# The first half of SwiGLU_1 in a staircase of four column groups, with the first two conditioning columns summed by TensorE

## The chip, the cores and the metric

The kernel runs on one core of one Trainium2 chip. The metric is device time in microseconds (us), the median of several runs; the time before is 1943.49 us (three runs, 1943.44 to 1944.72). The engines that matter are TensorE (PE, with its weight loads PEld), VectorE (DVE), ScalarE (ACT) and SyncE (SP), whose queue issues all DMA transfers. Each engine takes its instructions strictly in the order in which they stand in its queue. A scheduler fixes that order when the kernel is built; it is free to place instructions that do not depend on each other otherwise than the code writes them.

## The reference

One decoder layer on 256 tokens of width 2048 in float32. Only its first step is touched:

```python
mod = silu(c) @ ada_w + ada_b                  # 9 x 2048 numbers: shift, scale, gate of three stages
h = rmsnorm(x) * norm_g * (1 + sc1) + sh1      # 256 x 2048
x = x + 0.5 * gt1 * ((silu(h @ wg) * (h @ wu)) @ wd)   # wg, wu: 2048 x 5632, wd: 5632 x 2048
```

A mixer (two groups of heads), a second SwiGLU and a final norm follow.

## The kernel before, in words

Features lie on the 128 partitions: h is 16 tiles of 128 features x 256 tokens, numbered k = 0 to 15. Each of the two weight matrices wg and wu is cut into tiles of 128x128, k by f (f = 0 to 43 is a column of 128 hidden features). To keep float32 accuracy with the faster rounded type, each weight tile is split into a rounded part `whi` and a remainder `wlo`, and each h tile into a part HI and a part LO, so a weight tile costs three matmuls of 128x256: hi times HI (L567), hi times LO (L568), lo times HI (L569).

Weights arrive in blocks of eight tiles (512 KB, `Stream.block`, L112 to 124): SP issues the DMA into `wraw` (five buffers in this stage), ACT rounds it into `whi` (L123, four buffers), DVE subtracts to make `wlo` (L135, four buffers). A buffer of `whi` or `wlo` is free again when PE has read its last tile. The order in which `next` is called for tiles (L126) is the order of the blocks; the host packs them so.

The conditioning columns come the same way: a column is 128 output features of `mod`, 1 MB of `ada_w`; DVE multiplies it with silu(c) and sums it (L260, one custom instruction). Tile k of h needs two columns, scale and shift of its 128 features; then DVE multiplies x by the gain and the norm's row (`ht`, L368), ACT adds the shift and rounds (L375; L370 and L371 for odd k), and DVE makes the LO part (L376, L372). `RATE` says how many columns are loaded per block; `ada_need` forces a column that the code is about to use.

SwiGLU_1's gate and up products are made in two halves; the first half, 28 columns f, is `gate_up_first`. It makes them before all of h exists. A PSUM bank (of eight) holds g and u of one f. `CHUNKS` cuts the 16 tiles k into 0-1, 2-7 and 8-15; in each chunk a first group of eight f is worked k by k (`LEAD` says for how many k), then f by f, then the other f singly. When an f's chunk is finished its bank is emptied at once (`evacuate`): after the first chunk ACT copies it to an accumulator (L580), after the second DVE adds it (L582), after the third DVE adds gate and up to it for the activation (L585).

Before the first product stands a head, in which everything of the start is made: PE does ten warm-up matmuls on zeros, spreads c over the partitions by four one-row matmuls (`pcs`, L658), transposes x (`px`, L679), and turns the norm's reciprocal into a row (`nrow`, L709); ACT squares x (`junk`, L673), makes silu(c) (`cs`, L662) and copies PSUM to x (L681); DVE computes the reciprocal root and sums the first two columns, each in two halves (L694).

## Time and profile before

| what | value |
|---|---|
| median of three runs | 1943.49 us |
| profiled execution | 1943.79 us, its span 1941.9 us |
| PE busy | 1903.0 us, 98% of the span |
| DVE busy | 1554.0 us, 80% |
| ACT busy | 1041.2 us, 54% |
| first product of SwiGLU_1 (first L567) | starts at 22.52 us |
| last product of its first half (last L569) | starts at 336.8 us |
| DMA, mean over the span | 268 GB/s |

Busy time is the union of an engine's instructions; PE at 98% leaves little idle time, and nearly all of what the change can touch lies in the first 340 us. The time outside the span (1.9 us) is launch and end.

### The profile page before, as it was taken

Reading aid. Unit: us, or ns where it says so; the run is one execution under the profiler, and the core shown is the slowest. Engines: PE = TensorE matmul, PEld = TensorE weight load, DVE = VectorE, ACT = ScalarE, POOL = GpSimd, SP = SyncE. Lnnn points to the kernel's source line nnn. Section 1 sums busy time; section 2 is a strip of 40 time slices with the busy share of each in tenths; the row PEclk is TensorE's granted clock in tenths of the full one; section 3 lists DMA queues with packets and bytes.
Section 4 is the critical chain, followed back from the end, with each engine's and each line's share of the span. In section 5 each row is a group of like instructions: output and inputs, shape, how many; then the busy total and the mean of one; then the engine's idle time right before and its main releaser. Section 6 shows DMA issues by size and latency. Waiting matters only on the chain. (4 is left out here: it accounts for less than half of the span.)

```text
span 1941.9 us, 33701 instructions
## 1 busy us (share of the span) xinstructions
PE 1903.0 (98%) x13087; PEld 1777.2 (92%) x13087; DVE 1554.0 (80%) x2415; ACT 1041.2 (54%) x1647; POOL 56.8 (3%) x55
## 2 busy tenths in 40 slices
PE   8999999999999999999999999999999999999998
PEld 6999999998999988889989998999999999999997
DVE  6999978989989997779987989976777665666654
ACT  6544555433455446858657655665554445555553
POOL 0000000000000030000000001100000000000011
PEclk8999999999999999999999999999999999999999
DMA  9989867999999975586667568667767665565663
GB/s 371 359 308 358 305 224 258 400 369 376 356 358 339 361 302 212 212 314 220 214 242 257 201 218 303 208 258 252 245 253 257 244 225 200 201 200 202 202 200 120
DMA packets 129490, 519.58 MB, mean 268 GB/s; under 512 B 18217, under 2 KB 21545, under 8 KB 111153
## 3 DMA queue, kind: packets, MB, share of 16 engines
q1 hardware_dynamic: 129330, 517.42, 72.9%
q8 instruction: 103, 1.69, 0.3%
q14 instruction: 57, 0.47, 0.1%
HBM read 512.89 MB, written 4.47 MB: 266 GB/s over the span
## 5 line engine op out<-in xcount | busy, mean ns | idle before, releaser
L135 DVE TENSOR_TENSOR wlo<-wraw,whi 128x1024 fp32r<-128x1024 f32 x674 | 822.3, 1226 | 268.3 <-ACT whi L123 267.3
L123 ACT CAST whi<-wraw 128x1024 fp32r<-128x1024 f32 x674 | 700.6, 1047 | 515.1 <-PE pd L485 166.5
L485 PE MATMUL pd<-hid,whi 128*128 128x512 f32 x1408 | 461.8, 382 | 0.0
L486 PE MATMUL pd<-hid,wlo 128*128 128x256 f32 x1408 | 384.6, 273 | 2.6 <-DVE wlo L135 2.6
L260 DVE CUSTOM_DVE_ANT_0 adat<-adat,cs,colt 128x2048 f32<-128x2048 f32 x140 | 329.2, 2351 | 6.5 <-DMA adat<-in_ada_dram 6.5
L481 PE MATMUL pg<-hs,whi 128*128 128x512 f32 x912 | 302.2, 382 | 0.5 <-DVE shc L432 0.5
L481 PE MATMUL pu<-hs,whi 128*128 128x512 f32 x912 | 302.2, 382 | 0.0
L485 PEld LDWEIGHTS pd<-hid,whi 128*128 128x128 f32 x1408 | 266.0, 189 | 36.9
L486 PEld LDWEIGHTS pd<-hid,wlo 128*128 128x128 f32 x1408 | 270.3, 192 | 5.4 <-DVE wlo L135 5.3
L567 PE MATMUL pgu<-hs,whi 128*128 128x256 f32 x896 | 245.8, 277 | 5.9 <-ACT hs L371 5.9
L482 PE MATMUL pu<-hs,wlo 128*128 128x256 f32 x912 | 249.2, 273 | 0.0
L482 PE MATMUL pg<-hs,wlo 128*128 128x256 f32 x912 | 248.9, 273 | 0.0
L569 PE MATMUL pgu<-hs,wlo 128*128 128x256 f32 x896 | 245.1, 278 | 2.4 <-DVE wlo L135 2.4
L568 PE MATMUL pgu<-hs,whi 128*128 128x256 f32 x896 | 246.5, 277 | 0.0
L481 PEld LDWEIGHTS pg<-hs,whi 128*128 128x128 f32 x912 | 172.4, 189 | 24.8 <-ACT shc L431 0.7
L481 PEld LDWEIGHTS pu<-hs,whi 128*128 128x128 f32 x912 | 172.4, 189 | 23.6
L769 PE MATMUL pp<-hs,whi 128*128 128x256 f32 x656 | 188.9, 289 | 1.6 <-ACT hs L375 1.6
L770 PE MATMUL pp<-hs,whi 128*128 128x256 f32 x656 | 182.9, 279 | 0.0
L771 PE MATMUL pp<-hs,wlo 128*128 128x256 f32 x656 | 182.7, 278 | 0.0
L567 PEld LDWEIGHTS pgu<-hs,whi 128*128 128x128 f32 x896 | 172.9, 194 | 6.7 <-ACT hs L371 6.3
L482 PEld LDWEIGHTS pu<-hs,wlo 128*128 128x128 f32 x912 | 175.0, 192 | 1.0 <-DVE wlo L135 0.9
L482 PEld LDWEIGHTS pg<-hs,wlo 128*128 128x128 f32 x912 | 175.1, 192 | 0.4
(337 smaller groups left out, 2593.8 us busy)
## 6 DMA issues: line engine op xcount, KB each, us to landing
wraw<-in_w_dram SPq DMA_DIRECT2D x674, 512.0 KB, 4.4
adat<-in_ada_dram SPq DMA_DIRECT2D x140, 1024.0 KB, 7.2
xr<-in_xr_dram SPq DMA_DIRECT2D x4, 512.0 KB, 5.3
adaf<-in_ada_dram SPq DMA_DIRECT2D x4, 512.0 KB, 8.5
adaf<-in_ada_dram SPq DMA_DIRECT2D x2, 1024.0 KB, 12.3
xd<-x SPq DMA_DIRECT2D x4, 512.0 KB, 7.0
rw<-rowd SPq DMA_DIRECT2D x16, 128.0 KB, 4.3
x<-xd SPq DMA_DIRECT2D x4, 512.0 KB, 5.8
```

Source lines behind the costliest of these rows:

```text
L123: self.cast = self.nc.scalar.copy(self.h, r).ins
L135: lo_ = nc.vector.tensor_tensor(self.l, r, self.h.bitcast(F32), ALU.subtract)
L260: V.tensor_tensor_reduce(t, t, cs, 1.0, L("adab", q, 1), ALU.mult, ALU.add, mod[:, q : q + 1])
L481: PE.matmul(ps, wt[0], both, start=(k == 0), stop=False)
L482: PE.matmul(ps[:, T:], wt[1], part(k, HI), start=False, stop=(k == KD - 1))
L485: PE.matmul(ps, wt[0], act.rearrange("p q (a b) -> p q b a", a=2), start=first, stop=False)
L486: PE.matmul(ps[:, :T], wt[1], woven(act[:, 0]), start=False, stop=last)
L567: PE.matmul(o, wh, part(k, HI), start=first and s == 0, stop=False, skip_group_check=skip)
L568: PE.matmul(o, wh, part(k, LO), start=False, stop=False, skip_group_check=skip)
L569: PE.matmul(o, wl, part(k, HI), start=False, stop=last, skip_group_check=skip)
L769: PE.matmul(pp[i][:, :T], wh, hh, start=(k == 0), stop=False)
L770: PE.matmul(pp[i][:, :T], wh, hl, start=False, stop=False)
```

## The change

It has five parts.

1. `CHUNKS` and `LEAD` give way to `PIECES`, thirteen rows (group, first k, k up to which the group is worked k by k, end k) over groups of 8, 8, 8 and 4 columns f. The number of blocks is the same (112); the first blocks use k = 0 alone for two groups, the third group brings in k = 1, the fourth k = 2, and so on. There are 13 pieces where group and chunk gave 12; 28 banks are copied by ACT as before, 32 are added in the middle by DVE where there were 28.
2. A bank is no longer emptied when its piece is finished, but when the next piece asks for it (`owed`), except in pieces that end f by f.
3. Head: the first two columns (`first_col`) are summed by TensorE, sixteen 128x1 float32 matmuls each, with silu(c) as a column `csk` that sixteen one-row 128x1 matmuls `pct` prepare. The second half of `cs` is made after the first rounded weights; block 0 is rounded and subtracted in two halves; two and two warm-up matmuls stand where seven stood.
4. A later column is summed by DVE one block after the block with which it was loaded (`W.late`, `lag`), and `RATE` is 0.5 columns per block up to block 12 and then 0.45 up to block 68, where it was 0.5 up to 24, 0.34 up to 56 and 0.45 up to 68.
5. The rows of `ada_w` for the first two columns are packed so that TensorE can take them as stationary operand.

```diff
-CHUNKS = (0, 2, 8, 16)
-LEAD = (2, 5, 5)
+PIECES = (
+    (0, 0, 1, 1), (1, 0, 1, 1), (2, 0, 2, 2), (3, 0, 3, 3), (0, 1, 4, 4), (1, 1, 6, 6), (3, 3, 7, 7),
+    (2, 2, 11, 11), (3, 7, 12, 12), (0, 4, 11, 16), (1, 6, 6, 16), (2, 11, 11, 16), (3, 12, 12, 16),
+)
-RATE = ((0, 0.5), (24, 0.34), (56, 0.45), (68, 0.06), (112, 0.5), (168, 0.38), (264, 0.0), (284, 0.26), (404, 0.0), (424, 0.125))
+RATE = ((0, 0.5), (12, 0.45), (68, 0.06), (112, 0.5), (168, 0.38), (264, 0.0), (284, 0.26), (404, 0.0), (424, 0.125))
-N_WARM = (10, 7)
+N_WARM = (10, 2, 2)
...
-        self.cast = self.nc.scalar.copy(self.h, r).ins
+        with nullcontext() if b != 1 else self.tc.issue_after(self.lead):
+            one, *more = self.pieces(b)
+            h = self.h
+            self.cast = self.nc.scalar.copy(h[:, one], r[:, one]).ins
+            self.rest += [lambda q=q: self.nc.scalar.copy(h[:, q], r[:, q]).ins for q in more]
...
             with self.tc.issue_after(lo_.ins):
-                self.settle(b - BEHIND)
+                self.settle(b - self.lag)
...
-        for ci, (k0, k1) in enumerate(chunks):
...
+        for g, k0, ks, k1 in PIECES:
+            grp = fs[8 * g : 8 * g + 8]
+            pb = {}
+
+            def both(f, k):
+                ada_need(0, k)
+                if f not in pb:
+                    if len(owed) == 8:
+                        owed.pop(0)()
+                    pb[f] = bank()
+                for s in range(2):
+                    three(pb[f], f, s, k, k0, k1)
+
+            for k in range(k0, ks):
+                for f in grp:
+                    both(f, k)
+            for f in grp:
+                for k in range(max(k0, ks), k1):
+                    both(f, k)
+                owed.append(lambda f=f, ps=pb[f], k0=k0, k1=k1: evacuate(ps, f, k0, k1))
+                while ks < k1 and len(owed) > 1:
+                    owed.pop(0)()
+        while owed:
+            owed.pop(0)()
...
+    spread(0, psb)
+    spread(1, psb)
+    pct = psf("pct")
+    for k in range(KD):
+        PE.matmul(pct[:, k : k + 1], crow[:, k * P : (k + 1) * P], one[:1, :1], start=True, stop=True)
...
-    for kind, i in (("x", 0), ("x", 1), ("c", 0), ("c", 1), ("x", 2), ("x", 3), ("c", 2), ("c", 3)):
+    for kind, i in (("x", 0), ("x", 1), ("c", 0), ("c", 1), ("k", 0), ("x", 2), ("x", 3)):
...
+            elif kind == "k":
+                hold = A.activation(csk, pct[:, :KD], AF.Silu).ins
...
+        for k in range(KD):
+            PE.matmul(pcol[:, i : i + 1], first_ada[i][:, k * P : (k + 1) * P], csk[:, k : k + 1], start=(k == 0),
+                      stop=(k == KD - 1), skip_group_check=True)
+        return V.tensor_tensor(mod[:, q : q + 1], pcol[:, i : i + 1], L("adab", q, 1), ALU.add)
```

How the order moves on three engines follows. The first place is PE's queue in the head, between the ten warm-up matmuls and the first product. Before:

```order
L658 MATMUL pcs<-crow,one 128x512 x4
L679 MATMUL px<-colt,xr 128x128 x24
L709 MATMUL nrow<-colt,frb 128x128 x2
L679 MATMUL px<-colt,xr 128x128 x8
L201 LDWEIGHTS zw
L201 MATMUL zp<-zw 128x512
```

Now (`pct` is c as a column, `pcol` the sum of a conditioning column, `adaf_118` the first of the two; after these rows come one more warm-up matmul, the sixteen `pcol` matmuls of the second column `adaf_119`, two warm-up matmuls and the first product):

```order
L685 MATMUL pct<-one,crow 128x1 x16
L709 MATMUL px<-colt,xr 128x128 x12
L720 MATMUL pcol<-csk,adaf_118 128x1 x3
L709 MATMUL px<-colt,xr 128x128 x8
L720 MATMUL pcol<-csk,adaf_118 128x1 x5
L709 MATMUL px<-colt,xr 128x128 x5
L720 MATMUL pcol<-csk,adaf_118 128x1 x8
L736 MATMUL nrow<-colt,frb 128x128 x2
L709 MATMUL px<-colt,xr 128x128 x7
L679 MATMUL pcs<-crow,one 128x512 x2
L213 LDWEIGHTS zw
```

Forty-eight float32 matmuls of one column moved onto PE ahead of the first product, and two of the four `pcs` moved behind the norm's row.

The second place is ACT's queue from the first rounded h tile on (`whi` is a rounded weight block, `acc` the copy that empties a bank, `hs` the rounding of an h tile). Before:

```order
L375 ACTIVATE hs<-ht,mod 128x2x128
L123 CAST whi<-wraw 128x1024 x3
L370 ACTIVATE ht<-ht,mod 128x256
L371 CAST hs<-ht 128x2x128
L580 COPY acc<-pgu 128x512
L123 CAST whi<-wraw 128x1024
L580 COPY acc<-pgu 128x512 x3
L123 CAST whi<-wraw 128x1024
L580 COPY acc<-pgu 128x512 x5
L123 CAST whi<-wraw 128x1024
```

Now:

```order
L132 CAST whi<-wraw 128x512
L389 ACTIVATE hs<-ht,mod 128x2x128
L133 CAST whi<-wraw 128x512
L690 ACTIVATE cs<-pcs 128x512 x2
L132 CAST whi<-wraw 128x1024 x5
L598 COPY acc<-pgu 128x512 x4
L389 ACTIVATE hs<-ht,mod 128x2x128
L598 COPY acc<-pgu 128x512 x6
L132 CAST whi<-wraw 128x1024
L598 COPY acc<-pgu 128x512 x4
```

The rounding of h tile 1 moved from ahead of all bank copies to between the fourth and the fifth, and the first copy stands behind the rounding of block 5.

The third place is DVE's queue where a group of eight banks is emptied by additions for the first time. Before (the eight additions stand between the remainders of blocks 25 and 26; a pair of L260 rows is one column):

```order
L135 TENSOR_TENSOR wlo<-wraw,whi 128x1024
L372 TENSOR_TENSOR hs<-ht,hs 128x2x128
L135 TENSOR_TENSOR wlo<-wraw,whi 128x1024
L582 TENSOR_TENSOR acc<-pgu,acc 128x512 x8
L135 TENSOR_TENSOR wlo<-wraw,whi 128x1024
L260 ISA adat,mod<-adat,cs,colt 128x2048
```

Now (`wlo_928`, `wlo_963` and `wlo_994` are the remainders of blocks 18, 19 and 20; `pgu_679`, `694`, `701`, `708`, `715` are banks of f = 0 to 4):

```order
L146 TENSOR_TENSOR wlo_928<-wraw_924,whi_926 128x1024
L382 SCALAR_TENSOR_TENSOR ht_892<-x_85,g1_890,nrow_236 128x256
L600 TENSOR_TENSOR acc_363<-pgu_679,acc_363 128x512
L600 TENSOR_TENSOR acc_2634<-pgu_694,acc_2634 128x512
L395 SCALAR_TENSOR_TENSOR hs_127<-ht_892,mod_126,hs_127 128x2x128
L146 TENSOR_TENSOR wlo_963<-wraw_959,whi_961 128x1024
L272 ISA adat_930,mod_126<-adat_930,cs_86,colt_87 128x2048
L272 ISA mod_126 128x1
L146 TENSOR_TENSOR wlo_994<-wraw_990,whi_992 128x1024
L600 TENSOR_TENSOR acc_2636<-pgu_701,acc_2636 128x512
L600 TENSOR_TENSOR acc_2638<-pgu_708,acc_2638 128x512
L600 TENSOR_TENSOR acc_2640<-pgu_715,acc_2640 128x512
```

The additions are now split up: after two of them stand an h tile, two remainders and a column, then five more. On PE the products of the next piece that need the banks still to be emptied are placed behind those of block 19 for f = 8 and 9.

More of the change, by code (lines that the diff above doesn't have):

```diff
@@ L101, in __init__, with settle @@
         self.first = []
-        self.late, self.owing = False, []
-    def settle(self, upto=N_TILES):
+        self.lead, self.rest = None, []
+        self.late, self.owing, self.lag, self.pin = False, [], 1, None
+    def settle(self, upto):
         while self.owing and self.owing[0][0] <= upto:
-            self.owing.pop(0)[1]()
+            self.owing.pop(0)[2]()
     def behind(self, later=True):
@@ L272, in ada_need @@
             ada_col()
-        W.settle()
+        with nullcontext() if W.pin is None else tc.issue_after(W.pin):
+            while W.owing and W.owing[0][1] <= ada_seq.index((m, j)):
+                W.owing.pop(0)[2]()
     W.side = ada_col
@@ L374, in modulate_one @@
             with tc.issue_after(W.cast) if W.first else nullcontext():
-                A.activation(hh, tt, AF.Identity, bias=sh)
+                i = A.activation(hh, tt, AF.Identity, bias=sh).ins
+            if W.first:
+                for later in W.rest:
+                    with tc.issue_after(i):
+                        i = later()
+                W.lead = i
             return V.scalar_tensor_tensor(hl, tt, sh, hh.bitcast(F32), ALU.add, ALU.subtract)
@@ L557, in gate_up_first @@
         W.hold, W.held = None, [ada_done[0, 0]().ins]
-        groups = [fs[i : i + 8] for i in range(0, len(fs), 8)]
-        chunks = list(zip(CHUNKS[:-1], CHUNKS[1:]))
+        W.late = True
         acc, hids = {}, []
@@ L651, in ffn, with spread @@
             W.more = None
-    pcs = []
-    for q in range(4):
-        pcs.append(psn(q + 1, "pcs"))
+    pcs = {}
+    def spread(q, bank):
+        pcs[q] = bank("pcs")
         PE.matmul(pcs[q], one[:1], crow[:, q * 512 : (q + 1) * 512], start=True, stop=True)
+    spread(0, psb)
[3 more added lines that the diff above has]
+        PE.matmul(pct[:, k : k + 1], crow[:, k * P : (k + 1) * P], one[:1, :1], start=True, stop=True)
+    csk = ep.tile([P, KD], F32, name="csk")
     def cond(q):
@@ L711, in layer_kernel @@
     hold = A.copy(first_row, pr[:, :T]).ins
-    for i in range(4, KD // 2):
+    for i in (6, 7):
         features(i)
+    spread(2, pss)
+    spread(3, pss)
     with tc.issue_after(nr.ins):
         warm_up(N_WARM[1])
-    W.first.append(W.block(0))
-    first_col(0, 1)
-    first_col(1, 0)
-    first_col(1, 1)
+    first_col(1)
+    warm_up(N_WARM[2])
+    with tc.issue_after(hold):
+        W.first.append(W.block(0))
+    W.rest += [lambda q=q: cond(q) for q in (2, 3)]
     ada_st["i"] = 2
@@ L1244, in step @@
                     rowf[h + 1] = row_of(h + 1, 0, "f")
-        W.late = True
+        W.lag = 2
         first = project([("gt", 0)] + [("qkv", NH + h) for h in range(3)])
```

70 lines of the change are left out of this document (23 added, 47 removed).

## The prediction

> **What bounds the kernel now.** I read the page's first part, then stretches of the span, then what PE waits for, then the head in order of time.
>
> ```profile
> span 1941.9 us, 33701 instructions
> PE 1903.0 (98%) x13087; PEld 1777.2 (92%) x13087; DVE 1554.0 (80%) x2415; ACT 1041.2 (54%) x1647; POOL 56.8 (3%) x55
> ```
>
> PE bounds the span, so only its idle time and its slow stretches can be won or lost. The next view gives the busy time of each engine in some stretches; the last three columns are the granted clock, the share of the DMA engines and GB/s.
>
> ```profile
> 6.07:9.49 3.42, 3.42 (x9) 1.19 (x8) 0.00 (x0) 3.21 (x8) 0.00 (x0) 1.00 1.03 391
> 9.49:12.90 3.41, 3.41 (x17) 3.41 (x17) 1.53 (x4) 2.94 (x8) 0.00 (x0) 0.50 1.03 376
> 12.90:16.31 3.41, 1.06 (x10) 0.81 (x8) 3.31 (x12) 1.28 (x3) 0.00 (x0) 1.00 1.01 412
> 16.31:19.73 3.42, 2.56 (x12) 2.56 (x13) 2.62 (x9) 1.31 (x4) 0.00 (x0) 0.50 1.03 431
> 19.73:23.14 3.41, 3.41 (x11) 1.60 (x10) 1.00 (x2) 3.31 (x6) 0.00 (x0) 0.50 1.01 422
> 29.97:33.38 3.41, 1.28 (x9) 1.11 (x10) 3.41 (x5) 0.94 (x2) 0.00 (x0) 1.00 0.99 413
> 33.38:36.79 3.41, 3.41 (x19) 3.41 (x18) 3.19 (x5) 2.61 (x4) 0.00 (x0) 0.50 1.04 435
> 150.00:200.00 50.00, 50.00 (x450) 50.00 (x450) 49.07 (x58) 21.97 (x25) 0.00 (x0) 1.00 0.94 354
> ```
>
> In the last row 450 matmuls take 50 us: 0.111 us each, 2.67 us for a block (24). There DVE is busy 49 of 50 us, so it is a close second. The clock moves in steps of 3.41 us: after a stretch with little PE work (1.28 us) the next runs at half.
>
> ```profile
> L567 PE MATMUL pgu<-hs,whi x896: 275/275/765, 22.5 to 336.5; 128*128 128x256 f32 x180
> L569 PE MATMUL pgu<-hs,wlo x896: 274/275/423, 24.6 to 336.8; 128*128 128x256 f32 x180
> ```
>
> Three lines of 896 make 2688 matmuls, at 0.111 us 298.7 us; they take 336.8 + 0.3 - 22.5 = 314.6. **The first half loses 15.9 us, and its first product starts at 22.5 us.** These two numbers are what the change can alter. What PE waits for in the first 330 us, besides clock:
>
> ```profile
> PE pgu L567 <- ACT hs L371: 5.9, 2, 3.6
> PE pgu L569 <- DVE wlo L135: 2.4, 4, 1.5
> ```
>
> That is two h tiles that came late (3.6 and 2.3, with half clock behind them) and remainders `wlo` that came late.
>
> **The head: start of the first product.** From the order of time:
>
> ```profile
> 5.61 3.91 PE L658 MATMUL pcs<-crow,one 1*128 1x512 f32 x8
> 9.45 4.51 PE L679 MATMUL px<-colt,xr 128*128 128x128 f32 x24
> 18.18 1.92 PE L679 MATMUL px<-colt,xr 128*128 128x128 f32 x8
> 741.30 0.51 PE L323 MATMUL nsum<-colt,sqacc 128*128 128x2 f32 x4
> 10.12 1.06 ACT L673 ACTIVATE junk<-xr 128x1024 bf16<-128x1024 f32 x1 [0.47 <-DMA xr<-in_xr_dram]
> 11.08 0.18 ACT L673 ACTIVATION_READ_ACCUMULATOR junk<-xr 128x1 f32 x1
> 11.17 1.07 ACT L662 ACTIVATE cs<-pcs 128x512 f32<-128x512 f32 x2
> 12.13 2.05 ACT L681 COPY x<-px 128x512 f32<-128x512 f32 x4
> 18.42 0.37 ACT L711 COPY nrow<-nrow 128x256 f32<-128x256 f32 x1 [4.25 <-PE nrow L709]
> 11.83 1.28 DVE L694 CUSTOM_DVE_ANT_0 adaf<-adaf,cs,colt 128x1024 f32<-128x1024 f32 x1
> 16.63 0.16 DVE L292 SCALAR_TENSOR_TENSOR rsy_n<-rsa_n,rsy_n 128x2 f32<-128x2 f32 x1
> 16.82 0.48 DVE L708 TENSOR_SCALAR frb<-one,rsy_n 128x128 f32<-128x128 f32 x2
> 21.55 0.56 ACT L375 ACTIVATE hs<-ht,mod 128x256 fp32r<-128x256 f32 x1
> 22.52 1.10 PE L567 MATMUL pgu<-hs,whi 128*128 128x256 f32 x4
> ```
>
> A float32 matmul that is no transpose shows as two records (four `pcs` are eight). The four nsum records end 0.51 us after the first starts, of which one record's 0.25 is drain: about 0.11 us apart, though each has only two columns. A 128x1 matmul is then 2 x 0.11 = 0.22 us at full clock, and 0.43 at half (transposes go from 0.11 to 0.21: eight in 1.92 at half, with the last one's drain). That row is the nearest there is for `pct` and `pcol`.
>
> The Trainium skill, page "TensorE: Matmul & The Clock Gate", section "Back-to-back issue gap", gives a floor of about 25 ns between matmuls of at most 64 columns; the nsum row, four times that, decides here, as each record there brings its own weight load. By the page's floor a column would be 0.8 us in place of 3.6, and the sum would be that of rival (d), 1944.0.
>
> PE's queue, step by step: two `pcs` (four records of 0.43) end at 7.6. `pct`, 32 records, takes 3.6 us at full clock; but the row 6.07:9.49 shows that one-row matmuls that keep PE busy for 3.42 us leave the next stretch at half, so from 9.49 the other 16 take 3.4: end 12.8. Behind it stands ACT: silu of `csk`, which before did not exist, and behind that the last two squares (the last began at 10.12 before), which now end at 15.8 (from 13.4, 1.06 and most of a read each). The x copies at 0.51 follow and free banks from 16.3 on. PE meanwhile: 12 transposes to 15.4, three `pcol` to 16.6. From here the clock matters. At full: eight transposes as the copies free banks, 17.4; five `pcol` 18.5; five transposes 19.05; eight `pcol` 20.85; `nrow` 21.3 (DVE's eleven small operations of 0.19 from 15.9 on and the 0.48 behind them end at 18.5, hidden); seven transposes 22.1; two `pcs` 23.8; two warm-ups 24.25; sixteen `pcol` 27.8; then PE's drain and DVE's addition of the bias 0.45, and ACT's rounding 0.56: **first product at 28.8, 6.3 us later than before**. The same with full clock throughout (9.49 too) gives 27.0; with half clock from 16.6 on, 39.3 (8 and 5 and 7 transposes 4.3, 13 `pcol` 5.5, `nrow` 0.85, `pcs` 3.4, warm-ups 0.85, `pcol` 6.8, end 1.0). I take 28.8: a `pcol` loads weights in all 128 rows, where a `pcs` has one. Both ends stay for the range. The four half sums of 1.28 that DVE loses, 5.1 us, stood on this path too, between its small operations; that gain is in the times above, and PE's new work outweighs it.
>
> The Trainium skill, same page, section "Part 1: The HAM clock gate", says that the clock follows how busy PE has been; by it 27.0 would hold, 1.8 us less. The row 6.07:9.49 (all busy, half clock next) speaks against it.
>
> **After the start.** Durations, copies and additions of a bank first:
>
> ```profile
> L580 ACT COPY acc<-pgu x28: 568/587/619, 33.4 to 66.9; 128x512 f32<-128x512 f32 x28
> L582 DVE TENSOR_TENSOR acc<-pgu,acc x28: 682/688/697, 99.1 to 187.7; 128x512 f32<-128x512 f32 x28
> L123 ACT CAST whi<-wraw x674: 1027/1047/1093, 20.1 to 1919.0; 128x1024 fp32r<-128x1024 f32 x169
> 22.54 2.36 DVE L135 TENSOR_TENSOR wlo<-wraw,whi 128x1024 fp32r<-128x1024 f32 x2
> 24.81 2.35 DVE L260 CUSTOM_DVE_ANT_0 adaf<-adaf,cs,colt 128x2048 f32<-128x2048 f32 x1
> 30.57 0.48 DVE L368 SCALAR_TENSOR_TENSOR ht<-x,g,nrow 128x256 f32<-128x256 f32 x1
> 30.96 1.22 DVE L135 TENSOR_TENSOR wlo<-wraw,whi 128x1024 fp32r<-128x1024 f32 x1
> ```
>
> From start to start on DVE a remainder is 1.14 (two in 24.81 - 22.54), a column 2.27 (its next stands at 27.08), `ht` 0.39. Times now count from the first product.
>
> Blocks 0 and 1: the rounding of block 1 stands behind the second half of block 0 and two `cs` (0.53 + 1.06 + 1.05 = 2.65), its remainder is ready at 3.9; PE ends at 6.1 instead of 5.3: 0.8.
>
> Block 2 needs the bank of f = 0. Its copy stands on ACT behind the rounding of block 5, whose buffer PE frees only when it ends block 1: 0.1 + 1.05 + 0.59 + 0.1 = 1.9 of idle PE.
>
> Block 3 needs the fifth copy, behind the rounding of h tile 1. That needs `ht`, and DVE has ahead of it, from 2.65 on, five remainders 5.7, two columns 4.55, gain and `ht` 0.5: 13.4; rounding to 14.1, copy to 14.7. PE is through block 2 at 10.55: 4.1. Then ACT, with 16 copies (9.4) and the roundings of blocks 6 and 7 among them, is late twice more, 0.5 and 0.7.
>
> Block 17, where eight banks are to be added. Until then PE is not held up (h tiles 2 and 3 are ready 4 and 6 us early). Let PE end block 16 at 0. DVE's queue there: remainder 18, `ht`, two additions, an h tile, remainder 19, a column, remainder 20, addition 3: 8.6 us. Remainder 18 could begin at -4.2 (its buffers come free at -5.3), but a column keeps DVE until -3.1; so addition 3 ends at 5.5, at best 4.4. PE has f = 8 and 9 of blocks 17 and 19 to do, 2.7: idle 2.8 (1.7 at best). The eighth addition stands behind another remainder and column: 0.5 more. Likewise at block 27 (second addition behind a remainder, a column, a remainder: 5.2 after the first, PE has 1.3 of work and DVE 2.0 of lead) 1.9; at block 31 (addition 4 behind four remainders and a column) 2.3; at block 54, 1.9. Together 3.3 + 1.9 + 2.3 + 1.9 = 9.4. The bounds of this term: 0 if DVE leads by its four `wlo` buffers everywhere, 15 if each place costs what 17 does with its clock.
>
> Half clock: the gap of 4.1 is longer than the 2.1 us of idleness in 29.97:33.38, so one stretch of half clock, 1.7. The switch to the next product at 336 shows 1.1 of the 15.9 and stays.
>
> Sum after the start: 0.8 + 1.9 + 4.1 + 1.2 + 9.4 + 1.7 + 1.1 = 20.2 where there were 15.9: **4.3 lost**.
>
> Edits with one answer: `RATE` and the one-block lag move the same 30 columns on DVE; four more additions are 2.8 us of DVE, in the places above; on SP the column of h tile 1 stands two weight blocks later, hidden by the later start (the queue runs at a full DMA share from 6 us on). After the first half the order differs only locally; the largest wait for a remainder there is small, so I count 0, within 1 either way.
>
> ```profile
> PE pd L486 <- DVE wlo L135: 2.6, 9, 0.6
> ```
>
> **Sum.** 1943.8 (profiled execution; span 1941.9) + 6.3 + 4.3 = 1954.4; the median of the runs lies 0.3 lower: **1954.1**.
>
> **Rivals.** (a) The columns count as idle PE and the clock stays at half through the head: start 39.3, 10.5 later still, and 1.7 of half clock behind the start: 1966. For it speaks the one-row stretch; against it that weights are loaded in full. (b) The other side: the staircase pays. DVE, no longer asked for a column per block, leads by four buffers, the later additions cost nothing and the copies of blocks 2 and 3 alone remain: 1943.5 + 6.3 - 15.9 + (0.8 + 1.9 + 1.2 + 1.1) = 1938.9. It decides where h tile 1 is ready with the fourth copy (4.1 and 1.7 gone); below 5.7 us lost after the start the kernel is faster by more than 0.2%. DVE at 49 of 50 us speaks against it. (c) Idle time only moves, 15.9 as before: 1949.8. (d) A 128x1 matmul costs next to nothing: then the squares end at 11.3 as before, `nrow` can start at 14.5 (2.6 of DVE and the wait), and with it 0.5, seven transposes and `pcs` 2.5 to 3.2 and the end 1.0 the start is 18.5 to 19.2, 18.7 taken: 1943.5 - 3.8 + 4.3 = 1944.0. It decides below 0.1 us a matmul; the nsum row says 0.22.
>
> **Chances and range.** Forecast 0.52, (a) 0.24, (b) 0.08, (c) 0.12, (d) 0.04. A measurement of this kernel tells 0.2%, 3.9 us, from no change. Faster: (b), 0.08. Same: (d) and the low end of (c) and the forecast, 0.08. Slower 0.84. The likeliest case alone spans 1949 to 1960 (late additions 4 to 15); the range 1944 to 1968 takes in (a), (c) and (d) and leaves (b) out.
>
> **What would show it.** First product near 29 (39 under a, below 22 under d); `pct` from 7.6 to 12.8; after the start a PE gap of about 4 us released by a bank copy with h tile 1's rounding ahead of it, and gaps of 2 to 3 at 80, 110 and 125 us behind additions. Wrong would be a first product before 25 us, or no gap above 1.5 us after it.

## The result and the profile after

The changed kernel takes **1973.66 us** (median of four runs, 1972.12 to 1976.78); the kernel before took 1943.47 in the same series. The ratio is 1.0162, with a 95% interval of 1.0149 to 1.0175: slower by 1.6%, and 20 us more than forecast. Of two kernels below one run each took over 3000 us; their medians leave it out.

The first part of the page after: PE's busy time has grown by 25 us.

```profile
span 1973.9 us, 33932 instructions
PE 1928.0 (98%) x13180; PEld 1797.3 (91%) x13180; DVE 1551.2 (79%) x2414; ACT 1038.9 (53%) x1646; POOL 54.0 (3%) x55
```

Cut at the same borders of PE's work, the two profiled executions compare as follows. "Lost" is the length of the first half less the 298.7 us of its matmuls at full clock. Each column is a single execution.

| stretch | before | after | difference | forecast |
|---|---|---|---|---|
| start of the first product | 22.5 | 42.6 | +20.1 | +6.3 |
| lost in the first half | 15.8 | 19.8 | +4.0 | +4.3 |
| rest of SwiGLU_1 | 404.4 | 412.1 | +7.7 | 0 |
| mixer with its projection | 502.5 | 502.6 | +0.1 | 0 |
| second SwiGLU and end | 697.9 | 698.1 | +0.2 | 0 |

**The head.** PE in order of time after (start, length, line, tile, count, and in brackets the idle time ahead). There is no idle time to speak of:

```profile
1.23 4.45 PE L213 MATMUL zp<-zw 128*128 128x512 bf16 x10 [1.23 <-DVE zw L206]
5.61 3.78 PE L679 MATMUL pcs<-crow,one 1*128 1x512 f32 x4
9.18 6.82 PE L685 MATMUL pct<-one,crow 1*128 1x1 f32 x32
15.93 2.82 PE L709 MATMUL px<-colt,xr 128*128 128x128 f32 x12
...
30.42 3.78 PE L679 MATMUL pcs<-crow,one 1*128 1x512 f32 x4
34.13 1.03 PE L213 MATMUL zp<-zw 128*128 128x512 bf16 x2
34.95 6.83 PE L720 MATMUL pcol<-csk,adaf 128*128 128x1 f32 x32
...
42.58 0.80 PE L585 MATMUL pgu<-hs,whi 128*128 128x256 f32 x2
```

The 32 records of `pct` in 6.82 us are 0.213 apart, the last 32 of `pcol` too: the half-clock spacing, from beginning to end. The clock column (the last number but two) reads 1.00 over this head and must not be believed there: the trace holds its first record of the clock at 44.7 us, and what lies ahead of it is shown as full.

```profile
22.62:26.03 3.41, 3.41 (x18) 3.41 (x18) 0.00 (x0) 0.58 (x1) 0.00 (x0) 1.00 0.84 342
```

Eighteen records in 3.41 us are half clock; at 0.11 us there would be thirty. The profiled execution is the longest of the four. The other three are 1.2 to 3.7 us shorter, with mean granted clocks of 0.984 to 0.987, like the two profiled executions of this head below that start at 39.4 us (0.985 both); so they probably started near 39.4 us too.

**The first half.** What PE waits for, and behind it ACT's and DVE's rows at the longest wait:

```profile
PE pgu L585 <- ACT acc L598: 5.6, 1, 5.6
PE pgu L585 <- DVE acc L600: 5.3, 6, 2.3
PE pgu L587 <- DVE wlo L146: 0.3, 1, 0.3
```

```profile
49.18 1.04 ACT L132 CAST whi<-wraw 128x1024 fp32r<-128x1024 f32 x1 [1.39 <-PE pgu L586]
54.20 2.05 ACT L598 COPY acc<-pgu 128x512 f32<-128x512 f32 x4 [3.97 <-DVE mod L272]
...
51.81 2.35 DVE L272 CUSTOM_DVE_ANT_0 adaf<-adaf,cs,colt 128x2048 f32<-128x2048 f32 x1
54.08 0.08 DVE L272 DVE_READ_ACCUMULATOR2_ANT mod<- 128x1 f32 x1
```

The first bank copy waits 3.97 us with nothing ahead of it on ACT; it starts when DVE has summed column 3. PE's idle time is followed by one stretch of half clock (the third of these):

```profile
48.11:51.53 3.42, 1.15 (x11) 0.95 (x9) 3.42 (x4) 1.04 (x1) 0.00 (x0) 1.00 1.00 413
51.53:54.94 3.41, 0.11 (x1) 0.11 (x1) 3.41 (x5) 0.74 (x2) 0.00 (x0) 0.50 1.01 411
54.94:58.36 3.42, 3.42 (x16) 3.42 (x17) 1.31 (x3) 3.42 (x8) 0.00 (x0) 0.50 1.04 430
```

**The rest of SwiGLU_1.** What PE waits for there; before, it was 2.6 us in all:

```profile
PE pd L505 <- DVE wlo L146: 4.8, 9, 1.0
PE pu L501 <- DVE wlo L146: 1.2, 2, 0.9
PE pg L501 <- DVE wlo L146: 1.0, 2, 0.5
```

### The profile page after: what moved, and what is told of

The parts are those of the page before. It is cut to its first block, busy times and chain, and to the rows that moved or that the text cites. A ratio compares the mean times of both kernels' runs of the same rounds, so it can differ in the third digit from the quotient of the medians.

```text
span 1973.9 us, 33932 instructions
## 1 busy us (share of the span) xinstructions
PE 1928.0 (98%) x13180; PEld 1797.3 (91%) x13180; DVE 1551.2 (79%) x2414; ACT 1038.9 (53%) x1646; POOL 54.0 (3%) x55
## 4 chain that ended last, share of the span: by engine, by line
PE 71%; DVE 10%; issue 4%; ACT 3%; DMA 1%; SPq 0%; DVEq 0%; ACTq 0%
PE pd L504 14%; PE pg L500 10%; PE pu L500 10%; PE pd L505 7%; PE pg L501 5%; PE pu L501 5%; DVE wlo L146 4%; PE pgu L585 3%; PE pgu L586 3%; PE pgu L587 3%; DVE adat L272 3%; PE pp L799 2%; PE pp L800 2%; PE pp L801 2%; PE po L504 1%
## 5 line engine op out<-in xcount | busy, mean ns | idle before, releaser
L146 DVE TENSOR_TENSOR wlo<-wraw,whi 128x1024 fp32r<-128x1024 f32 (+1 forms) x675 | 822.2, 1222 | 281.1 <-ACT whi L132 279.2
L132 ACT CAST whi<-wraw 128x1024 fp32r<-128x1024 f32 (+1 forms) x674 | 700.7, 1046 | 530.4 <-PE pd L504 148.0
L272 DVE CUSTOM_DVE_ANT_0 adat<-adat,cs,colt 128x2048 f32<-128x2048 f32 x140 | 331.1, 2365 | 0.0
```

The source lines that it names most:

```text
L132: self.cast = self.nc.scalar.copy(h[:, one], r[:, one]).ins
L146: lo_ = nc.vector.tensor_tensor(self.l[:, q], r[:, q], self.h[:, q].bitcast(F32), ALU.subtract)
L272: V.tensor_tensor_reduce(t, t, cs, 1.0, L("adab", q, 1), ALU.mult, ALU.add, mod[:, q : q + 1])
```

## The experiments

Eighteen kernels were run, seventeen of them in several runs beside the kernel before; p_probe_widths was executed once, for its profile. All medians are in us; the ratio is to the kernel before in the same series, with its interval. "Start" and "lost" are those of the table above, in the profiled execution. The six kernels that are not listed have their figures where they are described.

| run | median | ratio | start | lost |
|---|---|---|---|---|
| changed kernel | 1973.66 | 1.0162 (1.0149 to 1.0175) | 42.6 | 19.8 |
| a_old_head | 1957.50 | 1.0082 (1.0067 to 1.0097) | 21.6 | 18.7 |
| b_head_alone | 1964.58 | 1.0121 (1.0106 to 1.0136) | 42.6 | 17.5 |
| c_no_lag_later | 1967.93 | 1.0135 (1.0117 to 1.0153) | 39.4 | 20.0 |
| ac_head_and_lag | 1949.13 | 1.0034 (1.0022 to 1.0047) | 21.8 | 18.7 |
| d_own_memory | 1949.91 | 1.0039 (1.0024 to 1.0054) | 22.2 | 18.5 |
| e_emptied_at_once | 1946.22 | 1.0021 (1.0012 to 1.0030) | 21.5 | 15.1 |
| g_own_memory_at_once | 1946.64 | 1.0023 (1.0014 to 1.0032) | 21.6 | 15.3 |
| h_staircase_alone | 1937.42 | 0.9973 (0.9963 to 0.9984) | 22.4 | 11.8 |
| k_new_rate | 1947.52 | 1.0022 (1.0013 to 1.0031) | 22.6 | 15.6 |
| l_lag_first_half | 1936.52 | 0.9964 (0.9951 to 0.9978) | 22.2 | 11.3 |
| n_best | 1936.91 | 0.9973 (0.9963 to 0.9984) | 22.5 | 11.5 |
| q_after_old_rate | 1970.37 | 1.0142 (1.0123 to 1.0160) | 39.4 | 18.5 |

### The head undone, and alone

a_old_head takes the head of before into the changed kernel; b_head_alone puts the changed head into the kernel before. In each the diff is that of part 3 and 5 of the change, once backwards:

```diff
-    for k in range(KD):
-        PE.matmul(pct[:, k : k + 1], crow[:, k * P : (k + 1) * P], one[:1, :1], start=True, stop=True)
...
+    first_col(0, 1)
+    first_col(1, 0)
+    first_col(1, 1)
```

> The changed kernel with the head of before (DVE sums the first two columns, four spreads of c, warm-ups 10 and 7, block 0 in one piece); staircase, banks emptied at next use, the new column rate and the one-block lag stay. Theory (the head alone costs the 20 us that its first product is later, and nothing that follows depends on it): first product near 22.5 us, 20 us less than the changed kernel, 1953.5. Rival 1 (the staircase lives on blocks and columns that the late start lets pile up, and loses more without it): first product near 22.5, but the first half loses over 25 us instead of 20, 1960 or more. Rival 2 (the staircase pays once it starts early): below 1948.

> The kernel before with the changed head alone (first two columns by TensorE, block 0 in halves, two and two warm-ups), the old order of chunks, old column rate and no lag. Theory: first product near 42.6 us, and 20 us later all the way, 1963.5. Rival (work of the old order piles up during the late start, so that its first waits for h tiles and remainders go): up to 10 us of the 20 come back, 1953 to 1958. Both heads agree on the start; a first product at 29 us would say that the clock in the head depends on what follows.

Both edits also touch the rounding of h tile 1, which the list of parts does not name (one ScalarE instruction, L389, in the changed head, two, L370 and L371, in the old one). The head undone takes off 16 us, the head alone adds 22.5. The theory held, though a_old_head's 1953.5 was missed by 4: the mixer with its projection took 506.2 us there and 502.6 in the changed kernel, for a reason that was not found. In b_head_alone the first half loses 1.7 us more than in the kernel before, so nothing of the late start comes back.

### Matmuls of one column, and the clock

f_probe_columns adds 64 float32 128x1 matmuls behind 1000 us of dense work:

```diff
+        pb = psb("probe")
+        for n in range(64):
+            PE.matmul(pb[:, n : n + 1], x[:, n % 8, : P], L("ones", 0, 1), start=True, stop=True)
```

> The kernel before, with 64 extra float32 128x1 matmuls (128 records) between the last down product and the sums of the final norm; their result is used by nothing, so the time is the kernel before's plus what they take. They follow 1000 us of dense products, so the clock is full when they begin. Theory G (matmuls of one column keep the records busy but do not count for the clock): records 0.11 us apart at first, then, 3.4 to 6.8 us in, 0.21 apart to the end: 20 to 25 us more than before. Rival (they count, and the clock in the changed head stayed low for another reason): 0.11 apart throughout, 14.2 us more.

It took 1969.57, 27.5 us more than the kernel before (ratio 1.0147, 1.0132 to 1.0162), 24.9 of them in the probe and the others at half clock behind it. Order of time, and stretches of 3.41 us with PE's busy time (first), and the clock:

```profile
1928.75 24.92 PE L1319 MATMUL probe<-colt,x 128*128 128x1 f32 x128
...
1928.75:1932.16 3.41, 3.41 (x30) 3.41 (x29) 1.32 (x3) 0.42 (x1) 0.00 (x0) 0.88 0.00 0
1932.16:1935.57 3.41, 3.41 (x17) 3.41 (x18) 0.00 (x0) 0.00 (x0) 0.00 (x0) 0.50 0.00 0
```

PE is 100% busy by its records, in the second stretch no other engine runs, and 2.6 us in the clock falls to half and stays there. p_probe_widths asks what does count:

```diff
...
+        dense()
+        probe(48, 64)
+        dense()
+        probe(32, P)
+        dense()
+        probe(16, 512, 1)
+        dense()
+        for m in range(8):
+            probe(4, 1)
+            dense(1)
+        dense()
+        for m in range(6):
+            probe(8, 1)
+            dense(1)
+        dense()
+        for n in range(64):
+            PE.transpose(pb[:, :P], x[:, n % 16, :P], ident)
```

> The kernel before with stretches of extra float32 matmuls ahead of the sums of the final norm, each behind 12 dense 128x512 matmuls (10 us): 48 of 128x64, 32 of 128x128, 16 of one row by 512 columns, 8 times four 128x1 and one 128x512, 6 times eight 128x1 and one 128x512, and 64 transposes of 128x128; their results are used by nothing. Theory G (the share of time in which columns stream through all rows counts for the clock): one row by 512 falls to half, the transposes and 128x128 stay full or nearly, 128x64 lies between; four to one (49% wide) stays full, eight to one (32%) falls to half. Rival (any matmul of more than a few columns counts, one row or not): only the stretches with 128x1 fall. In each the spacing of the records tells it: 0.11 us at full clock for the narrow ones, 0.21 at half.

The one execution took 2094.67 us. The stretches in order of time, of each mixture the first and the last round:

```profile
1936.58 10.83 PE L1326 MATMUL probe<-x 128*128 128x64 f32 x96
1957.60 7.31 PE L1326 MATMUL probe<-x 128*128 128x128 f32 x64
1975.14 24.29 PE L1326 MATMUL probe<-x 1*128 1x512 f32 x32
...
2011.30 0.95 PE L1326 MATMUL probe<-x 128*128 128x1 f32 x8
2023.57 0.95 PE L1326 MATMUL probe<-x 128*128 128x1 f32 x8
...
2035.62 1.84 PE L1326 MATMUL probe<-x 128*128 128x1 f32 x16
2057.11 3.41 PE L1326 MATMUL probe<-x 128*128 128x1 f32 x16
2073.38 7.20 PE L1344 MATMUL probe<-colt,x 128*128 128x128 f32 x64
```

Records of 64 columns are 0.11 us apart for 10.8 us, full clock, where something in between had been expected; 128 columns and the transposes likewise. One row of 512 falls from 0.43 to 0.85 apart. Four one-column matmuls to one of 512 columns keep 0.11 throughout; eight to one fall to 0.21. A record of 512 columns takes 0.43 us, so 64 columns are 0.05 us of streaming in 0.11, the mixtures 0.85 of 1.74 (49%) and 0.85 of 2.6 (32%). In these runs about half of the time with columns streaming through all 128 rows kept the clock full and a third did not; what the engine's records call busy, and whether weights fill all rows, did not matter. Whether the time of streaming counts or the number of multiplications, they do not tell apart.

All probes start from full clock; what raises it from half they do not show. Two rows do, in part. In the kernel before, the stretch 9.49:12.90 at half, filled with 17 transposes alone, was followed by one at full clock. In the changed head as c_no_lag_later ran it, transposes, columns and one-row matmuls alternate, and the recorded clock stayed at half from 7.79 to 41.93 us:

```profile
15.55:18.97 3.42, 3.42 (x20) 3.42 (x18) 2.04 (x12) 2.22 (x5) 0.00 (x0) 0.50 1.04 436
```

How much streaming it takes to raise the clock is left open.

### The lag behind the first half

c_no_lag_later sums columns at once behind the first half of SwiGLU_1:

```diff
+        W.late = False
+        while W.owing:
+            W.owing.pop(0)[2]()
         return hids
...
-        W.lag = 2
+        W.late, W.lag = True, 2
```

> The changed kernel, with the columns summed at once (no one-block lag) from the end of the first half of SwiGLU_1 up to the mixer; all else stays. Theory L (the 8 us that the rest of SwiGLU_1 lost come from the lag, which puts a column's 2.3 us of DVE at another place among remainders): 8 us less, 1965.6, and the waits of the down product for remainders fall from 10 to about 5 us. Rival D (they come from the weights, loaded at another phase of the SP queue after the late start): unchanged, 1973.7 within 2, waits for remainders near 10 us.

The rest of SwiGLU_1 took 405.2 us (412.1 with the lag), and PE's waits there are those of before again:

```profile
PE pd L505 <- DVE wlo L146: 2.7, 7, 0.6
```

Theory L held: the stretch lost its 6.9 us, though the median fell by 5.7 and not by 8. Of the 7.6 us between the two profiled spans 6.9 are this, and 3.2 an earlier start, 39.4, of the same head (the mixer's stretch gave 2.4 back):

```profile
1.23 3.87 PE L213 MATMUL zp<-zw 128*128 128x512 bf16 x10 [1.23 <-DVE zw L206]
5.03 1.98 PE L682 MATMUL pcs<-crow,one 1*128 1x512 f32 x4
6.85 5.95 PE L688 MATMUL pct<-one,crow 1*128 1x1 f32 x32
```

Here the ten warm-ups brought the clock up, `pcs` ran at 0.43 a record, and a part of `pct` at 0.11. The Trainium skill, page "TensorE: Matmul & The Clock Gate", section "What's actually happening", says that the window that measures the activity runs freely, so that the same kernel ramps differently from run to run; 4.45 and 3.87 us for the same ten matmuls agree.

### Both undone, then one thing at a time

ac_head_and_lag has both edits and is the base for three more:

> The old head (as in the run a_old_head) and no lag after the first half (as in c_no_lag_later) together; staircase, next-use evacuation, new column rate and the lag within the first half stay. If the two causes are independent: 1957.5 - 7.3 = 1950, some 8 us above the kernel before, of which about 5 in the first half. If the lag only cost time because the head was late: near 1957. It is also the base for the next three.

1949.13 for 1950 expected: the two are independent. d_own_memory loads columns 2 and 3 elsewhere than in the memory that the accumulators take over:

```diff
-N_FIRST = 4
+N_FIRST = 2
```

> ac_head_and_lag with columns 2 and 3 of the conditioning loaded into the pool of the later columns in place of the closed pool of the head, whose memory the accumulators take over. Theory M (the first bank copy waits 2.4 us for the sum of column 3 because its accumulator takes over the head's memory, which that sum still reads): the first copy starts right behind the rounding of block 5, the gap of 5.5 us at the third block falls to 2 to 3.5, with less half clock behind it: 3 to 5 us less than ac_head_and_lag, 1945 to 1947. Rival Q (the queue: copies stand behind the rounding of block 5 and of h tile 1, as the prediction had it): the wait is only split differently, 6 us in all, 1950.

ACT's rows, in d_own_memory, where ac_head_and_lag has a first copy at 32 us:

```profile
24.85 1.07 ACT L583 COPY acc<-pgu 128x512 f32<-128x512 f32 x2 [2.08 <-issue]
...
28.18 4.03 ACT L583 COPY acc<-pgu 128x512 f32<-128x512 f32 x8
```

```profile
PE pgu L570 <- DVE acc L585: 5.1, 4, 2.2
PE pgu L572 <- DVE wlo L136: 3.6, 5, 1.9
```

The gap of 5.6 us is gone, as M said, and with it the order of the queue: the copies now stand ahead of h tile 1. But the time is the same. Remainders are waited for instead, 3.6 us in place of 0.3, and the first half loses 18.5 us in place of 18.7. Both expectations were half right: the cause was M's, the price Q's. (In ac_head_and_lag the first copy starts at 32.49 us, when the sum of column 3 ends.)

e_emptied_at_once empties each bank when its piece is finished:

```diff
-                while ks < k1 and len(owed) > 1:
+                while owed:
                     owed.pop(0)()
```

> ac_head_and_lag with each bank emptied as soon as its piece is finished, in place of at next use (one condition). Theory (emptying at next use puts copies and additions so late in their queues that PE waits for them): the gaps behind additions (2.3, 1.1, 1.0 and some of 0.5 us) go, 4 to 6 us less, 1944 to 1946. Rival (emptied at once, the additions stand ahead of remainders that PE needs sooner): waits for remainders take their place, 1950 or more.

The waits for additions, 5.6 us, are gone, those for remainders rose from 0.3 to 3.7, and the first half loses 3.6 us less. Both together, g_own_memory_at_once, are no better than this one:

> Both edits of the two runs before on ac_head_and_lag. If both theories hold and the gaps are separate: 7 to 10 us less than ac_head_and_lag, 1940 to 1943, level with the kernel before or a little faster. If the two remove the same wait: the better of the two, 1944 to 1947.

### The staircase, the rate and the lag apart

h_staircase_alone has the old rate and no lag; k_new_rate and l_lag_first_half add one of them; n_best has the edit of d_own_memory.

```diff
-RATE = ((0, 0.5), (12, 0.45), (68, 0.06), ...
+RATE = ((0, 0.5), (24, 0.34), (56, 0.45), (68, 0.06), ...
...
-        W.late = True
```

> e_emptied_at_once with the column rate of before and no lag in the first half either: the staircase alone on the kernel before, banks emptied at once. Theory V (VectorE's work decides what the first half loses, and the order of the products little): 4 additions more than before, 2.8 us, so 1943 to 1946. Rival 1 (the staircase needs the new rate, as it asks for h tiles earlier): forced columns stand ahead of remainders, 1950 or more. Rival 2 (rate and lag are what cost, the staircase pays): below 1941.

> h_staircase_alone with the new column rate (0.45 columns per block up to block 68) and still no lag. If the rate costs what e_emptied_at_once lost against h_staircase_alone: 1944 to 1947, with some 3 us more waiting for remainders in the first half and 4 us more in the projection behind the mixer (2.8 to 3.3 us of waits there with the new rate, 0.7 with the old). If the lag does: 1937 to 1939. If half each: 1941.

> h_staircase_alone with the one-block lag in the first half alone (off behind it) and still the old rate. If the lag costs it: 1944 to 1947. If the rate does: 1937 to 1939. The projection behind the mixer should not lengthen, since the columns there are those of the old rate.

> h_staircase_alone with columns 2 and 3 in the pool of the later columns (the edit of d_own_memory). With the old rate its gap of 4.6 us at the third block, and the half clock behind it, is the largest that is left: if it is a wait of its own, 3 to 5 us less, 1932 to 1934. If, as in the pair ac_head_and_lag and d_own_memory, the waiting only moves: 1937 within 1.5.

So rival 2 of the first expectation was right, and the rate, not the lag, is what costs. The staircase, with banks emptied at once, is **faster than the kernel before by 0.27%** (0.16 to 0.37), and with the lag in the first half by 0.36% (0.22 to 0.49). The new rate costs all of it and more: 10 us, of which 3.8 in the first half and 4 in the projection behind the mixer; the rest lies in the mixer, which varies by itself. n_best moved its wait once more (11.8 to 11.5 lost). For the rate, the pair e_emptied_at_once and l_lag_first_half differ in nothing else. Waits of ACT and PE in the first half and of PE in the projection, new rate:

```profile
ACT whi L124 <- DMA wraw<-in_w_dram: 13.3, 8, 2.3
PE pgu L572 <- DVE wlo L136: 3.7, 3, 1.9
PE po L490 <- DVE wlo L136: 3.3, 2, 2.0
```

Old rate:

```profile
ACT whi L124 <- DMA wraw<-in_w_dram: 3.3, 2, 1.8
PE pgu L572 <- DVE wlo L136: 0.5, 2, 0.3
PE po L490 <- DVE wlo L136: 0.7, 1, 0.7
```

Weights come late in the first half, 10 us of waiting more (in the pair h_staircase_alone and k_new_rate 4.9). Why the projection waits longer was not followed up. In the changed kernel itself the rate costs little:

> The changed kernel with the old column rate, all else unchanged. If the rate costs there what it cost in the kernel that starts early: 10 us less, 1963.5. If the late start, which lets loads run ahead, has already paid for what the rate cost in the first half (the profile of the changed kernel shows no wait of ScalarE for weights there): only the 4.6 us in the projection behind the mixer come back, 1969.

1970.37, which the intervals do not tell apart from 1973.66, and in the profiles 1.3 us less lost, the mixer with its projection 502.3 for 502.6, and 3.2 from the start (39.4). The second expectation held for the first half; in the projection 4.0 us did come back (82.4 to 78.4), but the mixer ahead of it was 3.7 longer. That stretch varied from 419.7 to 424.9 us over all profiles, and why is left open.

### What sets the loss of the first half

Three kernels on g_own_memory_at_once: half of each column's sum left out, half of its load as well, and half of the load alone.

```diff
+        n = D // 2 if i < 36 else D
...
-                    nc.sync.dma_start(t, adaw[i])
+                    nc.sync.dma_start(t[:, :n], adaw[i][:, :n])
...
-                V.tensor_tensor_reduce(t, t, cs, ...
+                for _ in range(D // n):
+                    V.tensor_tensor_reduce(t[:, :n], t[:, :n], cs[:, :n], ...
```

i_half_sums has the smaller sum alone, o_half_loads also the smaller load, x_loads_alone (all of the lines above) sums what is loaded twice.

> g_own_memory_at_once with the conditioning columns of SwiGLU_1's first stage (2 to 35) summed over 1024 of their 2048 elements only, which leaves out half of each sum and takes 1.13 us off VectorE 34 times, 38 us in all; everything else, loads too, stays. Theory V (VectorE bounds the first half, so the waits only move when one of them is removed): the first half loses 4 to 6 us instead of 16, 1934 to 1937. Rival (the waits come from the order in the queues, from late banks or late weights): it loses 12 or more, 1943 to 1947.

> i_half_sums with only the half of each column loaded that is summed (columns 2 to 35, 0.5 MB less each, 17 MB in all); half of each sum is left out, as there. Theory W (columns that are loaded sooner than needed hold up the weight blocks behind them in SyncE's queue, so that ScalarE waits for weights, 11.0 us in g_own_memory_at_once and 5.3 in i_half_sums, and PE for remainders behind it): the first half loses 6 to 9 us instead of 13.2, 1937 to 1940, and ScalarE's waits for weights are gone. Rival O (the order in VectorE's queue, where an addition that must wait for its bank stands ahead of remainders): the first half loses 12 to 13.5 as before, 1943 to 1945.

> o_half_loads with VectorE's work put back: each of columns 2 to 35 is summed twice over the 1024 elements that are loaded (its value is not the reference's), 2.4 us as a whole one or a little more. With g_own_memory_at_once (all loads, all sums: 15.3 us lost in the first half), i_half_sums (13.2) and o_half_loads (2.1) it completes the square. Theory W (the loads decide, VectorE has room for its sums): 2 to 5 us lost in the first half, 1936 to 1939. Rival B (both are at their limit, so that either alone loses the time): 10 us or more lost, 1944 or more.

| us lost in the first half | whole sums | half sums |
|---|---|---|
| whole loads | 15.3 (1946.64) | 13.2 (1944.50) |
| half loads | 8.1 (1939.19) | 2.1 (1935.83) |

In brackets are the medians, which come from four series. Theory V (VectorE alone is the bound) fell: 31 us less of its busy time gained 2. The loads gain 7 to 11 in the first half, the sums 2 to 6, depending on the other (by the medians 7 to 9 and 2 to 3): both are close to their limit, the loads closer. So 8.1 lies between what W and B expected, and W alone is not the whole: in x_loads_alone ScalarE waits only 1.3 us for weights, and 8.1 are lost all the same. DVE's rows in i_half_sums show how the time is lost although DVE is idle 64 us of the first half:

```profile
95.00 1.36 DVE L586 TENSOR_TENSOR acc<-pgu,acc 128x512 f32<-128x512 f32 x2 [5.12 <-PE pgu L573]
...
100.76 2.48 DVE L586 TENSOR_TENSOR acc<-pgu,acc 128x512 f32<-128x512 f32 x4
103.16 2.35 DVE L136 TENSOR_TENSOR wlo<-wraw,whi 128x1024 fp32r<-128x1024 f32 x2
```

It waits 5.1 us for a bank that PE has not finished, with remainders queued behind; then it works through the additions, and PE waits for the remainders, 3.5 us at 101. Since half loads alone remove most such waits, the bank was late because weights were; that link is inferred.

j_columns_gpsimd moved seven columns' products to GpSimd:

```diff
...
+                if 4 < i < 34 and i % 4 == 3:
+                    s = tiny.tile([P, 1], F32, name="colsum")
+                    G.tensor_tensor(t, t, cs, ALU.mult)
+                    A.activation(t, t, AF.Identity, accum_out=s)
+                    A.activation(mod[:, q : q + 1], s, AF.Identity, bias=L("adab", q, 1))
```

> g_own_memory_at_once with seven of the columns (every fourth from the eighth on) multiplied by GpSimd and summed by ScalarE, which takes 7 x 2.27 = 16 us off VectorE and puts some 2 us each on ScalarE. Theory V: 6 to 10 us less than g_own_memory_at_once, 1937 to 1941, faster than the kernel before. Rival (GpSimd is slow, or holds up VectorE or the h tile that waits for the column): no gain or a loss, 1947 or more, with waits for h tiles in place of those for remainders.

1962.24, ratio 1.0108 (1.0091 to 1.0125). Groups by line (busy time, mean ns): one product takes GpSimd 4.96 us, and the mean of DVE's additions to h tiles (`hs`) rises to 1940 ns:

```profile
L264 POOL TENSOR_TENSOR adat<-adat,cs 128x2048 f32<-128x2048 f32 x7 | 34.7, 4962 | 189.9 <-DMA adat<-in_ada_dram 139.7 <-DVE ht L378 50.1
L386 DVE SCALAR_TENSOR_TENSOR hs<-ht,mod,hs 128x256 fp32r<-128x256 f32 x8 | 15.5, 1940 | 3.4 <-ACT hs L385 3.3
```

The same group in g_own_memory_at_once:

```profile
L380 DVE SCALAR_TENSOR_TENSOR hs<-ht,mod,hs 128x256 fp32r<-128x256 f32 x8 | 3.8, 480 | 3.3 <-ACT hs L379 3.3
```

The mean hides two kinds. Five of the eight still take 0.48 us; the other three began while a product ran on GpSimd and lasted until it was over, 3.60 to 4.78 us. Two column sums took 6.6 us in the same way. Six additions of a bank, which read one operand from PSUM, ran beside a product without being held, at 0.68 us each:

```profile
110.35 4.57 POOL L264 TENSOR_TENSOR adat<-adat,cs 128x2048 f32<-128x2048 f32 x1 [26.13 <-DMA adat<-in_ada_dram]
110.39 3.67 DVE L591 TENSOR_TENSOR acc<-pgu,acc 128x512 f32<-128x512 f32 x6
...
138.59 4.80 POOL L264 TENSOR_TENSOR adat<-adat,cs 128x2048 f32<-128x2048 f32 x1 [23.67 <-DMA adat<-in_ada_dram]
138.89 4.78 DVE L386 SCALAR_TENSOR_TENSOR hs<-ht,mod,hs 128x256 fp32r<-128x256 f32 x1
```

## Why the prediction was wrong

**The sum by parts.** Undone in sequence, by the ratios: head 0.80% (15.5 us), lag behind the first half 0.48% (9), emptying at next use 0.13% (2.5, at the edge of what the intervals tell), new rate 0.57% (11), and the staircase with the lag in the first half gains 0.36% (7): together the 1.62%. The prices depend on the order: the head alone costs 1.2%, the rate in the changed kernel at most 0.2%.

**The head, +6.3 forecast, +20.1 measured: the step that failed** is the clock from 16.6 us on, where the prediction took "full" for the reason that a `pcol` loads weights in all 128 rows. The probes show that this does not count: one-column matmuls let the clock fall however busy PE's records are. In the head the clock had to be raised from half, which no probe tried; there the spacing of the records shows that it stayed low up to the first product. The price of one, 0.22 at full and 0.43 at half, was right (two records of 0.213), and so were the order of the queue and the bound of 39.3 with half clock from there on: two executions started at 39.4. Rival (a) was thus the right one for the head, and the row 6.07:9.49, all busy and half clock next, was already evidence for it. The remaining 3.2 us of the profiled execution lie ahead of 16.6: the ten warm-ups did not raise the clock there (4.45 us for 3.87), and so `pcs`, which the prediction took at 0.43 a record, ran at 0.85, and all of `pct` at half. Rival (d) is refuted by the same spacing. The rule of the Trainium skill (page "TensorE: Matmul & The Clock Gate", section "Part 1: The HAM clock gate") that the clock follows busyness agrees with these runs only if busy means columns streaming through all rows.

**After the start, +4.3 forecast, +4.0 measured: right in size, half by accident.** The gap of "about 4 us released by a bank copy with h tile 1's rounding ahead of it" came as one of 5.6 (1.9 and 4.1 had been forecast, at blocks 2 and 3), but the copy waited for the sum of column 3 through reused memory, as d_own_memory shows; the order of ACT's queue that the prediction read was a consequence of it: with that wait gone, the copies stand ahead of h tile 1. The 9.4 us behind additions measured 5.3 in six waits (the longest 2.3 us, at 99 us), with another 1.7 of half clock after the longest. That they are due to emptying at next use is shown by e_emptied_at_once. The step "`RATE` and the one-block lag move the same 30 columns on DVE" costed the wrong resource: it is the loads that the rate brings forward, and in a kernel that starts early they cost 10 us, with the projection's 4. In the first half of the changed kernel, where loads run ahead during the late start, ScalarE has no wait for weights, and the rate costs 1.3 us.

**The rest, 0 forecast, +7.7 measured: the second step that failed.** "After the first half the order differs only locally", so "I count 0", gave the term no price: the lag stayed switched on, each column's 2.3 us of DVE came a block later among remainders, and c_no_lag_later takes the 7 us back. Without this term the time would have stayed within the stated range: rival (a), 1966, plus 7.7 is 1974, close to what was measured.

**Rivals (b) and (c).** (b)'s 1938.9 is passed by the staircase with the old head, the old rate and banks emptied at once (1937.42), but by another sum: it starts at 22.4 us and loses 11.8, where (b) had 28.8 and 5.0. As changed, the kernel was never that case. (c), that idle time only moves, is what the pairs ac_head_and_lag with d_own_memory (18.7 and 18.5 lost) and h_staircase_alone with n_best (11.8 and 11.5) show for the largest single wait.

## What to carry to other kernels

Before putting narrow matmuls on TensorE, ask what share of the time has columns streaming through all rows, not how busy the engine looks: here half was enough to keep the clock and a third was not, and at half clock one-column matmuls and one-row matmuls alike took twice the time. When a wait is found, ask what is late next: where loads and VectorE are both near their limit, removing one wait alone moved it. And a change of several parts should be tried in parts: here the staircase gained 7 us, and head, lag, late emptying and rate cost 38 between them.

## What the runs showed of the hardware

One row of 512 columns counts as little for the clock as one column over all rows: both fell to half within 3.4 us of full clock, to 0.85 and 0.21 us a record. 64 columns over all rows, at the same 0.11 us a record as one column, kept it full for the 10.8 us that were tried. Transposes alone kept it full for 7.2 us and, in the kernel before, raised it from half. GpSimd's product of 128x2048 float32 took 4.96 us in the mean; VectorE's instructions on SBUF operands that began while it ran were held until its end (one of 0.48 us took up to 4.78), additions from a PSUM bank were not. A tile that takes over the memory of a closed pool waits for the last reader of that memory. The trace names that reader (`mod L272`) as the releaser of a copy that has nothing else to do with it; for the same wait in ac_head_and_lag, 2.41 us, it names a DMA. Where a trace has no record of the clock yet, the clock column reads 1.00 (up to 44.7 us in the changed kernel); the spacing of the records tells it.
